# A two-layer decoder on one core: y laid down as it is read, gelus behind the next sines, the queries' modulation in portions, z products at attention's begin, splits one by one

## The chip, the cores and the metric

One core of a Trainium2 chip runs the whole program. The metric is the device time of one execution in microseconds; three runs of a kernel are compared by their median.

## The reference

A sequence of 1024 tokens of width 1024 goes through a state-space layer and an attention layer. In short form (`rms` normalises, `mod` gives shift, scale and gate as c's product with a weight):

```
h = rms(x) * (1 + scale_a) + shift_a
u, z = split(h @ w_in)
y = ssm(u) + D * u                  # 64 groups of 16 channels, 64 complex states each
y = gelu(y)
y = y * sigmoid(y @ w_glu + b_glu) * silu(z)
x = x + gate_a * (y @ w_out)
h = rms(x) * (1 + scale_kv) + shift_kv
k, v, f_logit = split(h @ kv_w);  k = head_rms(k);  F = cumsum(log_sigmoid(f_logit))
h = rms(x) * (1 + scale_b) + shift_b
q, z = split(h @ w_in_b);  q = head_rms(q) / 8
s = q @ k.T + F_q - F_k, causal;  o = softmax(s) @ v        # 16 heads of 64
x = x + gate_b * ((o * silu(z)) @ w_out_b)
```

All is float32.

## The kernel before

Every float32 operand of a large product is split into a high part (`hi`, `aH`, `w_hi`, `wvh`) and the rest (`lo`, `aL`, `w_lo`, `wvl`), and a product is three passes over PE: high by high, low by high, high by low. `split` does this: ACT copies the high part (L94), DVE or POOL subtracts (L102). Weights come in strips through `weight_strip`: SP loads `w_raw`, then it is split.

The program runs through stages. A warm-up of PE (`wu`, L267) stands ahead of the first data. Then come the products u and z of the first layer. The mixer goes over eight tiles of channels, `e` = 0 to 7, each with its taps, products by rotating factors, a scan on DVE, and the way back. In each turn of its loop `tables` gives cosine and sine of the next tile (two calls of ACT's Sin, L596 and L597, from a table that ACT must load), `rotate_back` turns the scan's result (DVE, L213), and `states_out` makes y of the tile on PE (`py`, L700 and L701), puts it through the gelu on ACT in two halves (L703, from another table) and writes it from POOL's queue to the DRAM tensor `y_d` (L704). Later the eight tiles are read back twice by SP, as `yl` for the products with w_glu (`pj_g`) and as `yt` for the gate. On the chip a tile has its 128 partitions as 8 groups of 16 channels and 8 positions of a chunk; `y_rows` reads them back in another order, channel by position:

```
y_d[e].rearrange("(i c) (g k) -> (c g) i k", c=GC, k=NCH)
```

After the products with w_out (`pj_o`), x stands in eight tiles of 128 channels. Then six jobs follow one another, `v0`, `v2`, `k0`, `k2`, `q0`, `q2`: each takes two strips of 256 columns of the weights for values, keys or queries, and makes eight tiles of 128 tokens from each (`tkps`, 24 products of PE per tile, in PSUM buffers `psa`, of which there are three). Values go to DRAM. Keys and queries get a norm by head: ACT squares (L955), DVE sums (L956), POOL takes the power (L957, L958), DVE multiplies (`hnt`, L960); then PE transposes four tiles (`trps`) and the result goes to DRAM in two parts. `modulated` makes the operands of a job from x: DVE normalises and scales (`hmod` or x itself, L184), ACT adds the shift and rounds (`aH`, L185), DVE gives the rest (`aL`, L186). For values and keys this is done at the values' start, for queries at the head of job `q0`. The scale and shift come from vector products on DVE (`gemv`, L141), one per tile of 128 weights that `mod_load` brings in, at every second tile of the jobs `v2` to `k2`.

`z_strips_b` makes the gate's products z of the second layer (`zb`). It is a generator: each `next` emits the three products of one k. Attention walks over 64 steps (16 heads, four blocks of 256 queries); `ahead` makes scores and softmax of a step two steps ahead (`sp`, `mx`, `pr`), `values` transposes the weights (`tp`), splits them (`pth` on ACT, `ptl` on DVE) and multiplies with v (`ov`); `ob` and `oc` collect a step's result. Between steps `some_fill` takes products from `z_strips_b`, and when these are done from `first_rows`, which makes the first output rows (`f`) and needs the gated heads split by `split_o`.

A scheduler orders the instructions of each engine from the order of the code; `tc.issue_after(x)` holds what stands in it behind the instruction x.

## Time and profile before

| | us |
|---|---|
| median of 3 runs | 1188.87 (1187.64 to 1189.01) |
| profiled execution | 1188.02 |
| its span | 1186.2 |
| PE busy | 1148.3 |
| DVE busy | 845.9 |
| ACT busy | 607.1 |
| POOL busy | 318.6 |

The span runs from the first to the last instruction of the profiled execution; the time has 1.8 us around it. Busy times are those in which an engine has an instruction under way, without register and semaphore work; PE is TensorE, DVE VectorE, ACT ScalarE, POOL GpSimd and SP the engine that issues most transfers.

### The profile page before, as it was taken

Reading aid. Unit: us, or ns where it says so; the run is one execution under the profiler, and the core shown is the slowest. Engines: PE = TensorE matmul, PEld = TensorE weight load, DVE = VectorE, ACT = ScalarE, POOL = GpSimd, SP = SyncE. Lnnn points to the kernel's source line nnn. Section 1 sums busy time; section 2 is a strip of 40 time slices with the busy share of each in tenths; the row PEclk is TensorE's granted clock in tenths of the full one; section 3 lists DMA queues with packets and bytes.
Section 4 is the critical chain, followed back from the end, with each engine's and each line's share of the span. In section 5 each row is a group of like instructions: output and inputs, shape, how many; then the busy total and the mean of one; then the engine's idle time right before and its main releaser. Section 6 shows DMA issues by size and latency. Waiting matters only on the chain.

```text
span 1186.2 us, 20506 instructions
## 1 busy us (share of the span) xinstructions
PE 1148.3 (97%) x7486; PEld 1017.5 (86%) x7486; DVE 845.9 (71%) x1713; ACT 607.1 (51%) x1141; POOL 318.6 (27%) x524
## 2 busy tenths in 40 slices
PE   8999999999999999899998999999999999999998
PEld 7688888888888887899997999988988889888786
DVE  7769899887789775934668764458788888887421
ACT  6655776666435323423233342237777776885210
POOL 2300000000000243211343354345555454543100
PEclk8999999999999999999999999989999999999999
DMA  9664566596975872255765473436456564741242
GB/s 360 212 195 118 135 174 170 149 233 196 328 245 198 295 239 86 101 194 181 230 193 176 163 228 109 124 125 143 108 126 137 113 137 101 155 90 45 97 160 72
DMA packets 108099, 197.09 MB, mean 166 GB/s; under 512 B 16832, under 2 KB 57984, under 8 KB 106464
## 3 DMA queue, kind: packets, MB, share of 16 engines
q1 hardware_dynamic: 101104, 174.17, 50.1%
q0 software_dynamic: 5152, 16.85, 3.7%
q10 hardware_dynamic: 1744, 4.77, 1.7%
q8 instruction: 59, 0.97, 0.4%
q14 instruction: 40, 0.33, 0.1%
HBM read 138.21 MB, written 46.27 MB: 156 GB/s over the span
## 4 chain that ended last, share of the span: by engine, by line
PE 77%; DVE 11%; ACT 7%; issue 3%; DMA 2%; SPq 0%; ACTq 0%; DVEq 0%
PE tkps L931 22%; PE pj_g L113 8%; PE u L261 7%; PE pj_o L113 6%; PE zb L113 6%; PE pj_f L113 5%; PE tp L1157 4%; PE ov L1163 2%; PE ov L1164 2%; PE z L261 2%; PE sp L1125 2%; PE f L113 2%; PE sp L1126 2%; ACT pr L1132 2%; DVE ptl L1160 1%
## 5 line engine op out<-in xcount | busy, mean ns | idle before, releaser
L931 PE MATMUL tkps<-wvh,aH 128*128 128x256 f32 (+1 forms) x768 | 219.7, 286 | 6.3 <-DVE hnt L960 3.1
L931 PE MATMUL tkps<-wvl,aH 128*128 128x256 f32 (+1 forms) x768 | 216.1, 282 | 0.0
L931 PE MATMUL tkps<-wvh,aL 128*128 128x256 f32 (+1 forms) x768 | 215.9, 281 | 0.0
L931 PEld LDWEIGHTS tkps<-wvh,aH 128*128 128x128 f32 x768 | 144.4, 188 | 8.0 <-ACT aH L185 3.8
L931 PEld LDWEIGHTS tkps<-wvl,aH 128*128 128x128 f32 x768 | 144.7, 188 | 0.3 <-issue 0.2
L931 PEld LDWEIGHTS tkps<-wvh,aL 128*128 128x128 f32 x768 | 144.2, 188 | 0.6 <-issue 0.2
L1134 POOL TENSOR_SCALAR pr<-pr,sm 128x128 f32<-128x128 f32 (+7 forms) x128 | 96.6, 762 | 85.4 <-DVE sm L1133 84.0
L1159 ACT ACTIVATE pth<-tp 128x512 fp32r<-128x512 f32 (+1 forms) x192 | 87.2, 489 | 55.9 <-PE ov L1163 32.2
L1132 ACT ACTIVATE pr<-pr,mx 128x128 f32<-128x128 f32 (+7 forms) x128 | 98.9, 773 | 24.3 <-DVE mx L1129 22.8
L1160 DVE TENSOR_TENSOR ptl<-tp,pth 128x512 fp32r<-128x512 f32 (+1 forms) x192 | 101.2, 551 | 10.5 <-ACT pth L1159 9.4
L94 ACT ACTIVATE w_hi<-w_raw 128x1024 fp32r<-128x1024 f32 x48 | 50.7, 1056 | 80.8 <-PE pj_f L113 28.6
L1129 DVE CUSTOM_DVE_ANT_0 pr<-sp,msk 128x512 f32<-128x512 f32 (+3 forms) x128 | 72.7, 569 | 23.1 <-PE tp L1157 20.3
L955 ACT ACTIVATE hsq<-tkps 128x256 f32<-128x256 f32 x64 | 24.6, 384 | 125.8 <-PE tkps L931 118.0
L1157 PE MATMUL tp<-ident,pr 128*128 128x128 f32 x576 | 84.9, 276 | 2.2 <-DVE ptl L1160 2.1
L1163 PE MATMUL ov<-pth,vhl 128*128 128x256 f32 x320 | 84.8, 298 | 0.3
L1164 PE MATMUL ov<-ptl,vhl 128*128 128x256 f32 x320 | 80.1, 284 | 1.8 <-DVE ptl L1160 1.7
L1157 PEld LDWEIGHTS tp<-ident,pr 128*128 128x128 f32 x576 | 69.4, 142 | 13.5 <-DVE ptl L1160 4.6
L1125 PE MATMUL sp<-kk,qs 128*128 128x256 f32 (+2 forms) x192 | 71.9, 377 | 2.6 <-DVE mx L1129 2.4
L958 POOL TENSOR_TENSOR hms<-hms,nhalf 128x4 f32<-128x4 f32 x64 | 67.8, 1060 | 5.3
L1126 PE MATMUL sp<-kk,q 66*128 66x256 f32 (+2 forms) x192 | 66.7, 351 | 0.0
L1163 PEld LDWEIGHTS ov<-pth,vhl 128*128 128x128 f32 x320 | 60.5, 189 | 3.2 <-DVE oc L1170 2.0
L1164 PEld LDWEIGHTS ov<-ptl,vhl 128*128 128x128 f32 x320 | 60.7, 190 | 3.0 <-DVE ptl L1160 2.8
(346 smaller groups left out, 3110.0 us busy)
## 6 DMA issues: line engine op xcount, KB each, us to landing
modw<-modw SPq DMA_DIRECT2D x48, 512.0 KB, 3.9
wvr<-kvq_w SPq DMA_DIRECT2D x12, 1024.0 KB, 5.7
w_raw<-a_w_in SPq DMA_DIRECT2D x16, 512.0 KB, 5.6
v_d<-vt POOLq DMA_DIRECT2D x32, 256.0 KB, 3.2
kk<-k_d SPq DMA_DIRECT2D x16, 512.0 KB, 6.6
vhl<-v_d SPq DMA_DIRECT2D x16, 512.0 KB, 8.2
qs<-q_d SPq DMA_DIRECT2D x32, 256.0 KB, 5.0
w_raw<-a_w_out SPq DMA_DIRECT2D x10, 512.0 KB, 5.4
```

The source lines that it names most:

```text
L113: m = T.matmul(ps, w[wt][:, k, :], act[at][k][half], start=(k == k0 and n == 0), stop=(k == k1 and n == 2)).ins
L261: m = T.matmul(ps[:, 0:c1 - c0], w[wt][:, k, :], act[at][k][i][:, c0:c1], start=(k == 0 and n == 0), stop=(k == KT - 1 and n == 2)).ins
L931: T.matmul(ps[:, 0:nv], at, wt[:, k, 0:nv], start=(n == 0), stop=(n == 3 * KT - 1))
L1125: T.matmul(sp[:, 0:wm_], qsl, kk[:, 0, lo:lo + wm_], start=True, stop=False)
L1126: T.matmul(sp[:, 0:wm_], q1_[:, P * i:P * i + P], kk[0:HD + 2, 1, lo:lo + wm_], start=False, stop=True)
L1132: S.activation(pr[:, 0:nk], pr[:, 0:nk], AF.Exp, scale=-1.0, bias=mx, accum_out=sm)
L1134: G.tensor_scalar(out=pr[:, 0:nk], in0=pr[:, 0:nk], scalar1=sm, scalar2=0.0, op0=ALU.mult, op1=ALU.add)
L1157: T.transpose(out=tp[:, b, :], in_=prs[qi][:, P * (b0 + b):P * (b0 + b) + P], identity=ident)
L1159: S.activation(pth[:, 0:m, dst], tp[:, 0:m, :], AF.Copy)
L1160: V.tensor_tensor(out=ptl[:, 0:m, dst], in0=tp[:, 0:m, :], in1=pth[:, 0:m, dst].bitcast(F32), op=ALU.subtract)
L1163: T.matmul(ov, vhl[:, b, :], pth[:, b - b0, :], start=(b == 0), stop=False)
L1164: end = T.matmul(ov, vhl[:, b, :], ptl[:, b - b0, :], start=False, stop=(b == nb - 1)).ins
```

## The change

- The warm-up has 38 calls instead of 28.
- `y_d` gets the order in which it is read. A tile is written in eight transfers of 16 partitions, each laid out by channel; the reads are plain. The first column of `r1` is cleared by DVE instead of POOL.
- `states_out` holds its gelus behind the sine of the next tile (`b_.get("sin")`), and behind them the table for sines is loaded ahead.
- `modulated` is cut into `mod_norm` and `mod_parts`. For the queries, two normalisations follow each tile of job `k2`'s first half, and the splits follow the tiles of `k2`'s second half and of `q0`'s first. The vector products follow every tile of `v2` and `k0`.
- The splits of `b_wz` wait for job `q0`'s end. The z products that stood among the queries and between the first scores are placed as 8 parts in `q2`, 5 behind each of the first two steps' scores and 3 behind each of the next two's.
- `first_rows` calls `split_o` once per part (three times at first) instead of all twelve at once, each behind the step's `ob` and `oc`.

```
-            for _ in range(28):
+            for _ in range(38):
...
-        y_d = dram.tile([KT, P, 8 * NCH], F32, name="y_d", tag="y_d")
+        y_d = dram.tile([KT, P, TC, NCH], F32, name="y_d", tag="y_d")
...
-            return y_d[e].rearrange("(i c) (g k) -> (c g) i k", c=GC, k=NCH)
+            return y_d[e]
...
-                S.activation(sT, sT, AF.Sin, scale=tpi)
+                st["sin"] = S.activation(sT, sT, AF.Sin, scale=tpi).ins
...
-                G.memset(r1[:, :, 0:1], 0.0)
+                V.memset(r1[:, :, 0:1], 0.0)
...
-                    S.activation(yb[:, 4 * hb:4 * hb + 4], py, AF.Gelu_apprx_tanh)
-                G.dma_start(out=y_d[e], in_=yb.rearrange("p g k -> p (g k)"))
+                    with tc.issue_after(sin) if sin else ExitStack():
+                        gelu = S.activation(yb[:, 4 * hb:4 * hb + 4], py, AF.Gelu_apprx_tanh).ins
+                if e + 2 < KT:
+                    with tc.issue_after(gelu):
+                        S.preload_act_table_set("trig_and_small")
+                for i in range(TC):
+                    G.dma_start(out=y_d[e, :, i, :].rearrange("(c g) k -> c g k", c=GC), in_=yb[GC * i:GC * i + GC])
...
             def z_strips_b():
-                w = weight_strip(a["b_wz"][0], [P, KT, P], l_eng=G)
+                with tc.issue_after(q0_end[0]), tc.issue_after(q0_end[1]):
+                    w = weight_strip(a["b_wz"][0], [P, KT, P], l_eng=G)
...
-                if job == "q0":
+                if job == "k2":
                     mod_take(last_nt[-1])
                     s_b = mod_scale(48, 56, vec["b_g"], "s_b")
...
-                    act = act_tiles()
-                    for i in range(2):
-                        for k in range(KT):
-                            with tc.issue_after(k0_end):
-                                modulated(x1, k, i, s_b, sh_b, act)
...
+                                with tc.issue_after(end), tc.issue_after(last_sq[-1]):
+                                    if job == "k2" and not i:
+                                        for ii in range(2):
+                                            mod_norm(x_half(n, ii), x_half(n, ii), ii, s_b[:, n:n + 1])
+                                    elif job == "k2":
+                                        mod_parts(x_half(n, 0), sh_b[:, n:n + 1], act_b[0][n][0], act_b[1][n][0])
+                                    elif job == "q0" and not i:
+                                        mod_parts(x_half(n, 1), sh_b[:, n:n + 1], act[0][n][1], act[1][n][1])
-                            if t % 2 and job != "v0":
+                            if job in ("v2", "k0"):
                                 mod_take(end, 1)
                                 mod_load(wide_dma[-1], 8 * KT)
...
-            for k in range(KT - 2):
-                for i in range(2):
-                    split_o(k, i)
+            todo = [(k, i) for i in range(2) for k in range(KT - 2)]
             for i in range(2):
                 ps = f_tile(0, i)
                 for k in range(KT - 2):
+                    for _ in range(3 if (k, i) == (0, 0) else 1):
+                        if todo:
+                            with tc.issue_after(ends[-1][1]), tc.issue_after(ends[-1][2]):
+                                split_o(*todo.pop(0))
                     project_part(ps, wf_(0), act2, i, (k,), 0, KT - 3)
...
         for j in range(LOOK):
-            if j:
-                some_fill(Z_FIRST)
             pend.append(ahead(j))
-        some_fill(Z_FIRST)
+            with tc.issue_after(sp_end[-1]):
+                some_fill(5)
...
+            if j < 2:
+                with tc.issue_after(sp_end[-1]):
+                    some_fill(3)
```

On ACT, near the end of the mixer's loop (`e` = 6; `r_2778` and `r_2836` are the tile's y before and after), the order before was:

```order
L595 ACTIVATE cT<-sT 128x1024
L703 ACT_TABLE_LOAD
L703 ACTIVATE r_2778<-py 128x512
L596 ACT_TABLE_LOAD
L596 ACTIVATE cT<-cT,hpi 128x1024
L597 ACTIVATE sT<-sT,tpi 128x1024
L703 ACT_TABLE_LOAD
L703 ACTIVATE r_2778<-py 128x512
L401 ACTIVATE ez_2818<-z_2_2819 128x32x8
```

and the changed kernel has there:

```order
L599 ACTIVATE cT<-sT 128x1024
L600 ACTIVATE cT<-cT,hpi 128x1024
L601 ACTIVATE sT<-sT,tpi 128x1024
L708 ACT_TABLE_LOAD
L708 ACTIVATE r_2836<-py 128x512 x2
L405 ACTIVATE ez_2883<-z_2_2884 128x32x8
```

The gelu that stood ahead of the cosine, and the two table loads around it, have gone from that place, and both halves stand behind the sine.

On DVE, at the step from keys to queries, this stood in the order before, the beginning of sixteen normalisations of x (`s_b` is the queries' scale):

```order
L956 TENSOR_REDUCE hms<-hsq 128x4
L163 TENSOR_TENSOR s_b<-mod,vecs 128x8
L168 SCALAR_TENSOR_TENSOR s_b<-s_b,vecs 128x8
L169 TENSOR_SCALAR s_b<-s_b 128x8
L184 SCALAR_TENSOR_TENSOR x_0_3167<-x_0_3167,s_b,q2x 128x512
L184 SCALAR_TENSOR_TENSOR x_1_3168<-x_1_3168,s_b,q2x 128x512
L184 SCALAR_TENSOR_TENSOR x_2_3169<-x_2_3169,s_b,q2x 128x512
L184 SCALAR_TENSOR_TENSOR x_3_3170<-x_3_3170,s_b,q2x 128x512
```

and in job `k2` of the changed kernel this (`hnt` is a finished tile of keys):

```order
L969 TENSOR_TENSOR hnt<-tkps,hms 128x256
L981 SCALAR_TENSOR_TENSOR kl<-trps,vecs,kh 128x512
L182 SCALAR_TENSOR_TENSOR x_4_3243<-x_4_3243,s_b,q2x 128x512 x2
L981 SCALAR_TENSOR_TENSOR kl<-trps,vecs,kh 128x512
L969 TENSOR_TENSOR hnt<-tkps,hms 128x256
L182 SCALAR_TENSOR_TENSOR x_5_3244<-x_5_3244,s_b,q2x 128x512 x2
L965 TENSOR_REDUCE hms<-hsq 128x4 x2
L969 TENSOR_TENSOR hnt<-tkps,hms 128x256
L182 SCALAR_TENSOR_TENSOR x_6_3245<-x_6_3245,s_b,q2x 128x512 x2
```

The normalisations have moved to an earlier job, and two of them stand between one tile and the next.

On ACT, in the last heads, the first splits of the gated heads (`aH`) stood like this before, from the step that was collected at 1016 us on:

```order
L1166 ACTIVATE ob<-ov 64x256
L94 ACTIVATE aH_0_12272<-o_t_7020 128x512
L94 ACTIVATE aH_0_12274<-o_t_7021 128x512
L1159 ACTIVATE pth<-tp 128x4x128
L1159 ACTIVATE pth<-tp 128x128
L1159 ACTIVATE pth<-tp 128x2x128
L1166 ACTIVATE ob<-ov 64x256
L94 ACTIVATE aH_0_12276<-o_t_8320 128x512
```

and stand like this in the changed kernel, eight steps later:

```order
L1193 ACTIVATE ob<-ov 64x256
L94 ACTIVATE aH_0_12344<-o_t_7412 128x512
L94 ACTIVATE aH_0_12346<-o_t_7413 128x512
L94 ACTIVATE aH_0_12348<-o_t_8392 128x512
L94 ACTIVATE aH_0_12350<-o_t_8393 128x512
L1186 ACTIVATE pth<-tp 128x4x128
L1159 ACTIVATE pr,sm<-pr,mx 128x640
L1186 ACTIVATE pth<-tp 128x128
```

Four splits stand in one piece ahead of the next step's `pth`, and DVE's halves (`aL`) stand likewise ahead of its `ptl`.

## Rows read from the trace of the kernel before

**Rows 1.** The page's first part: engine, busy us (share of the span), instructions.

```profile
PE 1148.3 (97%) x7486; PEld 1017.5 (86%) x7486; DVE 845.9 (71%) x1713; ACT 607.1 (51%) x1141; POOL 318.6 (27%) x524
```

**Rows 2.** The table of busy times by stretch of the span: from and to in us, length, then the busy time and count of instructions of PE, PEld, DVE, ACT and POOL, the granted clock of PE (1.00 is full), the share of the DMA engines and GB/s.

```profile
125.00:290.00 165.00, 154.41 (x1130) 138.23 (x1129) 142.03 (x168) 109.92 (x168) 5.14 (x15) 0.99 0.65 180
290.00:457.00 167.00, 167.00 (x725) 134.61 (x724) 126.13 (x173) 66.74 (x92) 21.80 (x21) 1.00 0.73 244
457.00:490.00 33.00, 28.69 (x153) 23.40 (x152) 30.68 (x36) 15.78 (x24) 13.42 (x13) 1.00 0.26 83
...
640.00:656.00 16.00, 10.47 (x71) 9.16 (x70) 16.00 (x27) 5.79 (x11) 4.16 (x4) 1.00 0.18 67
...
802.00:1017.00 215.00, 213.71 (x1398) 191.02 (x1396) 175.38 (x563) 161.70 (x384) 111.95 (x199) 1.00 0.59 129
1017.00:1053.00 36.00, 34.45 (x214) 29.15 (x213) 33.91 (x100) 29.38 (x69) 16.31 (x30) 1.00 0.46 103
1053.00:1072.00 19.00, 17.19 (x113) 15.02 (x112) 16.36 (x42) 13.65 (x29) 9.76 (x16) 1.00 0.38 85
1072.00:1112.00 40.00, 38.35 (x234) 32.35 (x234) 26.61 (x72) 21.80 (x50) 11.91 (x25) 1.00 0.15 46
```

**Rows 3.** The list of waits of PE over the whole span: what waited, what it waited for, us in total, times, the longest.

```profile
PE pk L641 <- DVE moa L213: 5.0, 6, 1.7
PE tkps L931 <- DVE hnt L960: 3.1, 1, 3.1
PE py L701 <- DVE r L213: 3.1, 3, 1.7
PE tkps L931 <- ACT aH L185: 2.8, 2, 1.5
PE sp L1125 <- DVE mx L1129: 2.4, 6, 0.7
PE zb L113 <- DVE aL L186: 2.4, 1, 2.4
```

**Rows 4.** The same kind of table as rows 2, cut where the granted clock changes.

```profile
9.81:12.51 2.70, 1.02 (x4) 0.66 (x4) 2.37 (x3) 1.92 (x4) 0.00 (x0) 1.00 1.02 410
12.51:19.34 6.83, 6.55 (x18) 4.56 (x17) 6.42 (x11) 5.67 (x8) 0.11 (x1) 0.50 1.03 410
...
131.97:135.38 3.41, 3.41 (x10) 2.63 (x9) 3.31 (x5) 2.20 (x6) 0.61 (x1) 0.50 0.79 302
790.00:794.16 4.16, 3.11 (x20) 2.25 (x19) 2.47 (x11) 2.05 (x6) 2.06 (x4) 1.00 0.00 0
794.16:800.98 6.82, 6.82 (x25) 5.59 (x25) 5.80 (x19) 4.94 (x13) 2.70 (x7) 0.50 0.67 231
```

**Rows 5.** The mixer: one row of the list of waits from 125 to 290 us, then rows of the timelines of ACT and of DVE around 265 us (start, length, engine, line, operation, in brackets the idle time before it and what ended it). L703 is the gelu, L596 the cosine, L213 a product on DVE.

```profile
DVE r L213 <- ACT cT L596: 9.7, 6, 4.4
...
262.63 1.28 ACT L703 ACT_TABLE_LOAD   x1
263.93 0.60 ACT L703 ACTIVATE r<-py 128x512 f32<-128x512 f32 x1
264.54 1.28 ACT L596 ACT_TABLE_LOAD   x1
...
267.02 1.22 DVE L213 TENSOR_TENSOR r<-cT,v 128x1016 f32<-128x1016 f32 x1 [4.36 <-ACT cT L596]
```

**Rows 6.** y on its way through DRAM: POOL's cleared columns (125 to 300 us), the time to landing in the view of y's DRAM tensor, and the last tile's write on POOL's timeline and its first read on SP's.

```profile
L677 POOL MEMSET r<- 128x8 f32 x7 | 0.8, 113 | 164.8 <-PE py L701 164.8
...
DMA to landing us min/median/max: 2.9/3.9/6.7
...
284.46 0.53 POOL L704 DMA_DIRECT2D y_d<-r  x1 [13.69 <-ACT r L703]
...
287.40 0.37 SPq L787 DMA_DIRECT2D yl<-y_d  x1
```

**Rows 7.** Groups of instructions from 463 to 490 us, on POOL and on DVE: line, engine, operation, tiles, shape, count | busy us, mean ns | idle before.

```profile
L102 POOL TENSOR_TENSOR w_lo<-w_raw,w_hi 128x1024 fp32r<-128x1024 f32 x2 | 4.8, 2398 | 3.4 <-ACT w_hi L94 3.3
...
L184 DVE SCALAR_TENSOR_TENSOR hmod<-x,s_kv,q2x 128x512 f32<-128x512 f32 x10 | 13.9, 1428 | 0.0
```

**Rows 8.** The step from keys to queries: a group on DVE from 636 to 656 us, and rows of PE's timeline.

```profile
L184 DVE SCALAR_TENSOR_TENSOR x<-x,s_b,q2x 128x512 f32<-128x512 f32 x16 | 10.9, 745 | 0.0
...
645.66 0.39 PE L931 MATMUL tkps<-wvh,aH 128*128 128x256 f32 x1 [3.11 <-DVE hnt L960]
...
648.58 0.27 PE L967 MATMUL trps<-ident,hnt 128*128 128x128 f32 x1
```

**Rows 9.** Groups on DVE from 500 to 640 us, values and keys.

```profile
L141 DVE CUSTOM_DVE_ANT_0 modw<-modw,c_b 128x1024 f32<-128x1024 f32 x16 | 19.4, 1210 | 0.0
...
L956 DVE TENSOR_REDUCE hms<-hsq 128x4 f32<-128x256 f32 x21 | 8.7, 417 | 8.0 <-ACT hsq L955 7.9
L960 DVE TENSOR_TENSOR hnt<-tkps,hms 128x256 f32<-128x256 f32 x20 | 8.4, 421 | 11.7 <-POOL hms L958 11.5
...
L972 DVE SCALAR_TENSOR_TENSOR kl<-trps,vecs,kh 128x512 fp32r<-128x512 f32 x8 | 5.6, 747 | 0.7 <-ACT kh L971 0.7
```

**Rows 10.** A group on DVE from 990 to 1121 us: the splits of the gated heads.

```profile
L102 DVE TENSOR_TENSOR aL<-o_t,aH 128x512 fp32r<-128x512 f32 x16 | 12.4, 783 | 2.9 <-ACT aH L94 2.8
```

**Rows 11.** A group on PE from 0 to 41 us: the warm-up.

```profile
L267 PE MATMUL wu<-onesm 128*128 128x128 f32 x56 | 8.7, 331 | 1.1 <-POOL onesm L66 1.1
```

More of the change, by code (lines that the diff above doesn't have):

```diff
@@ L102, in split, with act_tiles @@
             parts[:] = h, (l_eng or V).tensor_tensor(out=lo, in0=x, in1=hi.bitcast(F32), op=ALU.subtract)
-        def act_tiles(more=0):
-            return [[[apool.tile([P, HL + more * i], F32R, name=f"a{p}{k}_{i}", tag=f"a{p}{k}_{i}") for i in range(2)]
-                     for k in range(KT)] for p in "HL"]
+        def act_tiles(more=0, halves=(0, 1)):
+            return [[[apool.tile([P, HL + more * i], F32R, name=f"a{p}{k}_{i}", tag=f"a{p}{k}_{i}") if i in halves else None
+                      for i in range(2)] for k in range(KT)] for p in "HL"]
         def project_part(ps, w, act, half, ks, k0=0, k1=KT - 1):
@@ L1029, in trunk, with x_half @@
                     V.tensor_scalar(out=gate_b, in0=gate_b, scalar1=0.5, scalar2=None, op0=ALU.mult)
-                    act = act_tiles()
-                    for i in range(2):
+                elif job == "q0":
+                    act = act_tiles(0, (1,))
+                    for p in range(2):
                         for k in range(KT):
-                            with tc.issue_after(k0_end):
-                                modulated(x1, k, i, s_b, sh_b, act)
-                    lx.close()
-                    modx.close()
-                    at0 = top.enter_context(tc.tile_pool(name="at0", bufs=2, side="right", reuse_waits="tile"))
-                    o_t = [at0.tile([P, L], F32, name=f"o_t{e}", tag=f"o_t{e}", bufs=1) for e in range(2)]
+                            act[p][k][0] = act_b[p][k][0]
+                def x_half(k, i):
+                    return x1[k][:, HL * i:HL * i + HL]
                 src = a["kvq_w"]
@@ L1042, in trunk @@
                 for i in range(2):
+                    if job == "k2" and i:
+                        act_b = act_tiles(0, (0,))
+                    elif job == "q0" and i:
+                        lx.close()
+                        modx.close()
+                        at0 = top.enter_context(tc.tile_pool(name="at0", bufs=2, side="right", reuse_waits="tile"))
+                        o_t = [at0.tile([P, L], F32, name=f"o_t{e}", tag=f"o_t{e}", bufs=1) for e in range(2)]
                     for d in range(2):
@@ L1175, in trunk @@
             steps += [(2 * p + h, c) for h, c in ORDER]
-        hds = {}
-        ocs = {}
+        hds, ocs, sp_end = {}, {}, []
         def ahead(j):
```

46 lines of the change are left out of this document (25 added, 21 removed).

## The prediction

> **What bounds the kernel now.** I read the page first, for the busy shares: PE works 1148.3 us of the 1186.2 us span, 97% [rows 1]. So PE is the bound, and a change that leaves PE's work alone can give back at most what PE does not do: 37.9 us of idle time, and the work that it does at the lower clock. Next I read the table by stages, for where those 37.9 us lie [rows 2]: the reader is to see that the mixer's stretch from 125 to 290 us has 10.6 us of them (165 less 154.41) and the start of the values 4.3 us (33 less 28.69), that the sixteen us around the step from keys to queries have 5.5 us with DVE busy for all 16.00, and that the last heads (1017 to 1072) have 3.4 us. From 290 to 457 PE has none. Third, PE's list of waits, for who ends them [rows 3]: nearly always DVE, with one late operand each. Last, the granted clock [rows 4]: three stretches at 0.50, that is 1.2 instead of 2.4 GHz: 6.83 us at the first products, 3.41 us in the mixer, 6.82 us at the first scores. PE had waited just before: 1.68 us of idle time in the 2.70 us ahead of the first, 1.05 in the 4.16 us ahead of the last.
>
> The sum starts from the profiled execution, 1188.02 us; the median of the runs, 1188.87, lies 0.85 us above it.
>
> **The longer warm-up.** 28 calls are 56 passes of 8.7 us [rows 11], 0.155 us each, so ten more calls are 3.1 us. They cover the idle 1.6 us behind the warm-up and run 1.5 us into the time when the first data are there. What follows is paced by DVE, which is busy 6.42 of the 6.83 us at the low clock [rows 4], so a faster PE there mostly waits. Bounds: 1.5 us lost (the delay is not caught up), 1.5 us gained (the idle time saved). I take 0.5 us gained.
>
> **y laid down as it is read.** One write per tile becomes eight; the sixteen reads have long pieces instead of pieces of 128 elements. POOL issues such a transfer in 0.53 us [rows 6], so eight take 4.2 us and the last is issued 3.7 us later than the single one was. POOL has nothing else to do there. The write of tile 7 is what counts: it was issued at 284.46 us, and SP asked for the tile at 287.40 [rows 6]. The seven tiles ahead give PE products to do, and from 290 us PE never waited [rows 2]; how much slack tile 7 had, no row says. Bounds: 0, and 3.7 us lost. I take 0, for the shorter read gives part of it back. The cleared column (0.113 us, eight times) goes from POOL to DVE: 0.9 us, counted in the next part.
>
> **Gelus behind the next sines.** This is the largest term. In the mixer DVE waited 9.7 us in six places for ACT's cosine [rows 5]. The last place shows why: ACT loads a table (1.28 us), does a gelu (0.60), loads the sines' table (1.28) and only then the cosine, while DVE stands for 4.36 us. With the gelu behind, 3.16 us of this go, and 1.2 stay. The other five waits together are 5.3 us, some 1.1 each, less than those 3.16, so I let them go wholly. DVE gains 9.7 - 1.2 = 8.5 us, less the 0.9 us of the cleared columns: 7.6. The number of table loads stays at 19; a load for the sines now stands behind the gelu in ACT's order, ahead of the next evictions. PE gets what it waited for DVE: pk 5.0 and py 3.1 us [rows 3] of the 10.6 idle in the stretch, and the 3.41 us at half clock cost it 1.7 at most. Bounds: 2.5 us (only the first and largest waits turn into PE time, as gelus and loads delay the evictions of z) and 8.5 us. I take 6.0, some four fifths of DVE's 7.6, as PE and DVE don't wait at the same places throughout.
>
> That first row of ACT's also bears on a price. A load began at 262.63 and the gelu at 263.93: 1.30 us from one to the other [rows 5]. The Trainium skill ("ScalarE: Activation LUTs", What ACT_TABLE_LOAD costs) gives a drain of some 1.38 us beside the load, 2.66 us per switch. By that the two switches and the gelu would be 5.9 us, the last wait would go wholly as well, and the sum would be some 1 us lower. The rows show no room for such a drain.
>
> **The start of the values.** Two splits of the z weights leave: ACT's share, and on POOL two of 2.40 us each, while DVE's normalisations beside them average 1.428 us [rows 7] against 0.745 for the same form elsewhere [rows 8]. Ten at that difference are 6.8 us of DVE, some of it beside other POOL work that stays. PE waited 2.8 us for aH here, which hangs on these [rows 3]. I take 2.7 us, nearly all of it; bounds 1.5 and 4.3 (all idle time of the stretch).
>
> **The queries' modulation in portions.** Before, 16 normalisations in one piece (10.9 us of them inside the stretch [rows 8]) stand on DVE ahead of the tile that PE waits for: 3.1 us for hnt and 2.4 us for aL [rows 3], with all of DVE's 16.00 us taken [rows 2]. Now two come behind each tile of k2's first half and the splits behind the next two half jobs. A tile is 24 products, 2.9 us from the first to the transposes behind it (645.66 to 648.58) [rows 8]. DVE's work per tile is then 0.42 (squares' sum), 0.42 (hnt), 1.49 (two normalisations) and about 0.4 for kl [rows 9]: 2.7 us, just under the tile, and the weights' split comes to that; three PSUM buffers take up a lag of a tile. The same holds for k0, where the vector products of 1.21 us now follow each tile. I take 5.0 of the 5.5 us, bounds 3 and 5.5.
>
> **z products at attention's begin.** The number of products is unchanged. Instead of filling the queries' jobs, they stand between the first scores, where PE waited for mx: 1.05 us of idle time from 790 to 794.16, and 6.82 us ran at half clock [rows 3, 4], worth 3.4 us if PE alone was the bound. DVE was busy 5.80 of those 6.82. I take 1.0 + 2.5 = 3.5 us, bounds 0 (the clock falls at another place) and 4.4.
>
> **Splits one by one.** Here the order speaks against the change. Before, twelve splits stood singly or in pairs over 1017 to 1053 us, where PE lost 1.55 us; two heads without them lose some 0.2 [rows 2]. So 1.3 us come back. But now they wait for the step before the first product that needs them, and stand four, two, two, two and two behind one another within the five steps that were at 1058 to 1082 us, beside the split of a weight. Each takes DVE 0.78 us [rows 10]: 9.4 us. DVE's free time there: 2.64 us in 19 and 13.4 in 40 [rows 2], so about 1.9 + 3.3 = 5.2 in these 24. Over 4 us don't fit; scores run two steps ahead, which hides some 2.4 of them. I take 1.8 lost less 1.3 gained: 0.5 us lost. Bounds: 1.3 gained, 2.8 lost.
>
> **The sum.** -0.5 + 0 - 6.0 - 2.7 - 5.0 - 3.5 + 0.5 = -17.2, so 1170.8 us against 1188.02, and 1171.6 on the scale of the runs' median. A measurement tells about 0.2% from no change here, 2.4 us.
>
> **Rivals.**
> - *The mixer and the clock keep what they have.* The gelus and loads behind the sines hold the evictions of z instead, and the low clock only moves: 2.5 instead of 6.0 and 0 instead of 3.5, so 1171.6 + 7.0 = 1178.6. For it: ACT is busy 109.92 of 165 us there, and just as many loads remain. Against it: PE's long waits name DVE. Chance 0.17.
> - *The stall of the values' start moves along.* POOL's two splits of 2.40 us now stand in q2 between the powers that hnt waits for, and PE waits again: 2.7 given back, 1174.3. Against it: a tile's lag of 2.8 us fits into the PSUM buffers. Chance 0.08.
> - *All idle time goes.* 1.5, 8.5, 4.3, 5.5, 4.4 and 1.3 gained: 25.5, so 1163.4. Chance 0.09.
> - *Slower: the pieces of tile 7 land one after another.* If each of the eight holds up the next for a landing, the tile comes 7 landings later: at the median of 3.9 us [rows 6] that is 27.3 us, so 1171.6 + 27.3 = 1198.9. It decides from 2.8 us per piece (7 of them make the 17.2 and 2.4 more). Against it: POOL's issue takes 0.53 us of the 2.9 to 6.7 that a landing takes [rows 6], and the next issue needs nothing from the one before. Chance 0.05. The Trainium skill ("DMA: Bandwidth & Descriptors", Rules for kernel authors) speaks on this side: small transfers should be made one, as under 64 KB most of the time is overhead. A piece here is just 64 KB, so by that rule each would keep most of its fixed cost; no run yet shows whether these costs lie beside each other.
> - *It doesn't do what it says:* the gains and the new crowding at the end cancel, within 0.2% of before. Chance 0.04.
>
> **How the numbers follow.** The forecast, 1171.6 us, has 0.57, with a range of its own from 1166 to 1177. For 8 in 10 I go from 1162 to 1181, which takes in the first three rivals. Faster 0.91, the same 0.04, slower 0.05.
>
> **What would show it.** Right: DVE's wait for the cosine falls below 2 us, no PE wait over 1 us from 640 to 656, none for aH at the values' start, a clock of 1.00 at the first scores, PE's idle time near 22 us. Wrong: PE waits for ez's buffers in the mixer, an idle PE at the first product with y's tile 7, PE waits of more than 2 us for ptl in heads 13 and 14.

## The result, and the profile after

The changed kernel takes 1182.09 us (median of five runs, 1181.67 to 1183.26) against 1188.87 us: a ratio of 0.9945, with a 95% interval from 0.9929 to 0.9960. (Here and below the ratio is estimated from all executions of both kernels, so it need not be the quotient of the two medians.) That is faster, by some 0.55%: 6.8 us where 17.2 were forecast, and the median lies 1.1 us above the upper end of the range of 8 in 10, 1181. The profiled execution took 1183.26 us, its span is 1181.1 us, 5.1 us less than before's.

The page's first part of after (engine, busy us, share, instructions), to lay beside [rows 1]:

```profile
PE 1146.0 (97%) x7506; PEld 1018.0 (86%) x7506; DVE 838.3 (71%) x1721; ACT 605.6 (51%) x1141; POOL 349.8 (30%) x572
```

PE has 2.3 us less and DVE 7.6 us less; POOL has 31.2 us more, mainly the 56 more issues of y's pieces. The table by stages of after, with the columns of [rows 2]:

```profile
125.00:290.00 165.00, 153.11 (x1122) 137.54 (x1121) 140.48 (x173) 108.13 (x166) 32.29 (x62) 0.99 0.70 177
457.00:490.00 33.00, 31.86 (x178) 26.80 (x177) 27.11 (x38) 15.12 (x24) 10.25 (x11) 1.00 0.20 72
640.00:656.00 16.00, 16.00 (x138) 16.00 (x138) 11.54 (x23) 5.25 (x12) 6.49 (x10) 1.00 0.31 118
656.00:790.00 134.00, 129.82 (x1023) 125.90 (x1022) 66.86 (x136) 50.40 (x93) 59.65 (x89) 0.99 0.47 146
790.00:802.00 12.00, 12.00 (x71) 10.45 (x70) 9.04 (x32) 8.22 (x21) 5.44 (x9) 1.00 0.54 134
1053.00:1072.00 19.00, 15.17 (x86) 12.32 (x85) 17.32 (x42) 12.25 (x27) 9.74 (x14) 0.91 0.19 55
```

Read against [rows 2], the first number behind the length (PE busy) tells the story. Three stages did what they should: at the values' start PE's idle time is 1.1 instead of 4.3 us, from 640 to 656 us it is nothing instead of 5.5, and the first scores have neither idle time nor a low clock. Three others got worse: the mixer has 11.9 us idle instead of 10.6, the stretch from 656 to 790 has 4.2 us where there was none, and the last heads have 3.8 us in 19 instead of 1.8. The row of before from 656 to 790 us, which [rows 2] leaves out:

```profile
656.00:790.00 134.00, 134.00 (x1087) 131.19 (x1086) 71.47 (x135) 42.83 (x76) 58.14 (x85) 1.00 0.49 154
```

PE's list of waits names the new ones, with the columns of [rows 3]:

```profile
PE py L705 <- DVE r L217: 7.4, 5, 4.3
PE sp L1151 <- DVE mx L1156: 3.9, 4, 1.8
PE tkps L940 <- DVE hnt L969: 3.3, 2, 2.7
```

The single rows on PE's timeline of after (start, length, engine, line, operation, in brackets the idle time ahead and what ended it), one from each of the three stages:

```profile
280.91 0.80 PE L705 MATMUL py<-r,moa 128*128 128x128 f32 x2 [4.34 <-DVE r L217]
...
679.92 0.52 PE L940 MATMUL tkps<-wvh,aH 128*128 128x256 f32 x1 [2.67 <-DVE hnt L969]
...
1064.86 0.44 PE L1151 MATMUL sp<-kk,qs 128*128 128x384 f32 x1 [1.84 <-DVE mx L1156]
```

Within 0.9 us of the end of each of the three waits the granted clock falls to 0.50, which is 1.2 GHz. A table of after, cut there (the last row is the stretch of the first data, which had 6.83 us at 0.50 in [rows 4]):

```profile
280.50:284.20 3.70, 3.29 (x16) 3.29 (x17) 1.56 (x3) 0.61 (x1) 0.00 (x0) 0.54 0.57 173
680.00:683.30 3.30, 3.30 (x16) 3.30 (x17) 2.69 (x5) 0.00 (x0) 1.71 (x3) 0.50 0.04 12
1065.50:1069.30 3.80, 3.80 (x13) 3.26 (x14) 2.82 (x12) 3.09 (x9) 2.64 (x5) 0.55 0.51 173
17.80:21.30 3.50, 3.50 (x11) 2.92 (x12) 3.50 (x8) 2.80 (x5) 0.00 (x0) 0.51 1.04 411
```

So the low clock did not go; it moved from the first scores to these places, behind the new waits. It did shrink: before had four stretches of it, 20.5 us in all (a fourth, from 56.88 to 60.29 us, is not in [rows 4]), after has four of 3.4 us, 13.7 in all.

A ledger shows where the time went in one profiled execution of each kernel. Each row is a point in the program, read from the timelines: for before the time at which it is reached, for the others the difference to before in us (negative is earlier). "Scan e" is the end of DVE's scan for tile e, the others are starts on PE or ends on DVE. The columns e5 to e8 belong to the experiments below.

| point | before | after | e5 | e6 | e7 | e8 |
|---|---|---|---|---|---|---|
| scan 0 | 109.14 | +0.80 | -0.24 | -1.16 | +0.33 | -0.60 |
| scan 4 | 203.87 | -3.88 | -4.92 | -5.68 | -3.62 | -5.48 |
| scan 6 | 251.08 | -2.90 | -3.94 | -4.53 | -2.52 | -4.23 |
| scan 7 | 273.01 | -2.38 | -4.50 | -5.11 | -2.88 | -3.46 |
| last `py` | 283.26 | +2.49 | -1.40 | +0.14 | -0.50 | -2.86 |
| last `pj_o` | 473.23 | +2.48 | +3.02 | +2.82 | -0.50 | -2.04 |
| last tile of values | 573.66 | -1.90 | -1.30 | -1.55 | -4.97 | -6.35 |
| `oc` of step 8 | 845.28 | -7.54 | -7.17 | -9.78 | -10.64 | -14.39 |
| `oc` of step 42 | 1006.38 | -7.62 | -7.19 | -9.80 | -10.66 | -14.43 |
| end | 1186.25 | -5.10 | -4.72 | -6.21 | -12.66 | -16.46 |

After gains 3.9 us up to scan 4 and is 2.5 us late when the mixer ends: it gives back 6.4 us in the last three turns. DVE's waits in the mixer (125 to 292 us of after, columns as in the list of waits) say what for:

```profile
DVE sT L217 <- DMA v<-v: 10.9, 5, 6.5
...
DVE r L217 <- ACT cT L600: 1.2, 1, 1.2
```

The wait for the cosine fell from 9.7 us to 1.2 [rows 5], exactly as worked out. In its place stands `v<-v`, the transfer that exchanges the two halves of the scan's result: 10.9 us, where before it was 3.3 us in one place. Before's row of the same list, and the place on DVE's timeline of before:

```profile
DVE sT L213 <- DMA v<-v: 3.3, 1, 3.3
...
277.54 1.23 DVE L213 TENSOR_TENSOR sT<-sT,v 128x1024 f32<-128x1024 f32 x1 [3.27 <-DMA v<-v]
```

The two places that count, and the one cosine left, on DVE's timeline of after:

```profile
256.20 1.23 DVE L217 TENSOR_TENSOR sT<-sT,v 128x1024 f32<-128x1024 f32 x1 [3.24 <-DMA v<-v]
...
264.24 1.22 DVE L217 TENSOR_TENSOR r<-cT,v 128x1016 f32<-128x1016 f32 x1 [1.15 <-ACT cT L600]
...
278.38 1.23 DVE L217 TENSOR_TENSOR sT<-sT,v 128x1024 f32<-128x1024 f32 x1 [6.48 <-DMA v<-v]
```

The 3.2 us won at the last tile's cosine (4.36 in [rows 5], now 1.15) were lost 8 us earlier, on the 3.24 us of a swap that had not been waited for. At the last tile the swap takes 6.48 us instead of 3.27, and the half clock behind it costs some 1.7 more (an estimate: half of the 3.42 us at 0.50): 3.2 and 1.7 are the 4.9 us by which the ledger falls from scan 7 to the last `py`. The queue that issues the swap, SP's timeline of after:

```profile
266.27 0.53 SPq L408 DMA_DIRECT2D z_d<-ez  x1
267.17 0.94 SPq L796 DMA_DIRECT2D yl<-y_d  x2
268.20 0.37 SPq L86 DMA_DIRECT2D w_raw<-a_w_glu  x1
270.66 1.22 SPq L587 DMA_DIRECT2D v<-v  x2
```

Two reads of y and a strip of w_glu, 512 KB each, are issued 3.5 to 2.5 us ahead of the swap. Before, one read of y and the strip went out at 268.61 and 269.07 us, 4.4 and 4.0 us ahead of a swap at 273.04 (SP's timeline of before):

```profile
268.61 0.37 SPq L787 DMA_DIRECT2D yl<-y_d  x1
269.07 0.66 SPq L86 DMA_DIRECT2D w_raw<-a_w_glu  x1
273.04 1.16 SPq L583 DMA_DIRECT2D v<-v  x2
```

The scan moved forward by more than the loads, so the swap now comes closer behind 1.5 MB, where 1.0 MB stood further ahead.

### The profile page after: what moved, and what is told of

It reads as the page before. It is cut to its first block, busy times and chain, and to the rows that moved or that the text cites. A ratio compares the mean times of both kernels' runs of the same rounds, so it can differ in the third digit from the quotient of the medians.

```text
span 1181.1 us, 20618 instructions
## 1 busy us (share of the span) xinstructions
PE 1146.0 (97%) x7506; PEld 1018.0 (86%) x7506; DVE 838.3 (71%) x1721; ACT 605.6 (51%) x1141; POOL 349.8 (30%) x572
## 4 chain that ended last, share of the span: by engine, by line
PE 73%; DVE 9%; ACT 7%; DMA 6%; issue 3%; POOL 1%; SPq 0%; ACTq 0%; DVEq 0%
PE tkps L940 22%; PE pj_g L113 8%; PE pj_o L113 7%; PE zb L113 6%; PE pj_f L113 5%; PE u L265 5%; PE tp L1184 4%; PE ov L1190 3%; DMA v<-v 3%; PE ov L1191 2%; PE sp L1151 2%; PE sp L1152 2%; PE f L113 2%; ACT pr L1159 1%; ACT w_hi L94 1%
## 5 line engine op out<-in xcount | busy, mean ns | idle before, releaser
L713 POOL DMA_DIRECT2D y_d<-r x64 | 33.4, 552 | 200.2 <-ACT r L708 199.1
L967 POOL TENSOR_TENSOR hms<-hms,nhalf 128x4 f32<-128x4 f32 x64 | 70.8, 1106 | 5.3
L265 PE MATMUL z<-aH,w_hi 128*128 128x258 f32 (+2 forms) x192 | 62.7, 327 | 1.4 <-ACT ez L405 1.4
```

The lines of the kernel that those rows point to most:

```text
L265: m = T.matmul(ps[:, 0:c1 - c0], w[wt][:, k, :], act[at][k][i][:, c0:c1], start=(k == 0 and n == 0), stop=(k == KT - 1 and n == 2)).ins
```

## The experiments

The theory that came out of the ledger: the mixer's gain is real, and is given back by the last swap, late because of SP's order, with the clock behind it. Its rivals: the eight pieces on POOL's queue make the swap late; or the gelus' move is itself worth nothing. Of the queries' and the last heads' new waits the theory is that the order of PE's products and the crowding on DVE make them.

Each kernel is the changed one with the edit shown. They were timed in three groups, each beside runs of the kernel before on the same chip (medians 1189.16, 1189.14 and 1189.21 us): e1 to e4, e5 to e8, and e9 to e12, each group on a chip of its own. Medians of different groups are therefore compared with some care.

| kernel | median us | ratio to before, interval |
|---|---|---|
| after | 1182.09 | 0.9945 (0.9929 to 0.9960) |
| e1 y in one write | 1182.76 | 0.9942 (0.9922 to 0.9962) |
| e2 gelus as before | 1185.51 | 0.9965 (0.9948 to 0.9981) |
| e3 both | 1182.83 | 0.9942 (0.9922 to 0.9963) |
| e4 splits as before | 1181.72 | 0.9931 (0.9909 to 0.9953) |
| e5 swap first | 1181.06 | 0.9931 (0.9911 to 0.9950) |
| e6 queries' splits in twos | 1181.79 | 0.9938 (0.9923 to 0.9954) |
| e7 e4 and a split on POOL | 1176.95 | 0.9905 (0.9887 to 0.9923) |
| e8 e5, e6 and e7 | 1172.96 | 0.9867 (0.9848 to 0.9885) |
| e9 e8, mixer as before | 1176.97 | 0.9882 (0.9857 to 0.9908) |
| e10 e8 without e5 | 1175.51 | 0.9881 (0.9858 to 0.9903) |
| e11 e8, y in one write | 1174.00 | 0.9865 (0.9840 to 0.9890) |
| e12 e8, warm-up of 28 | 1172.60 | 0.9858 (0.9835 to 0.9881) |

**e1, y in its old layout and one write.**

```
-        y_d = dram.tile([KT, P, TC, NCH], ...)
+        y_d = dram.tile([KT, P, 8 * NCH], ...)
-            return y_d[e]
+            return y_d[e].rearrange("(i c) (g k) -> (c g) i k", c=GC, k=NCH)
-                for i in range(TC):
-                    G.dma_start(out=y_d[e, :, i, :]..., in_=yb[GC * i:GC * i + GC])
+                G.dma_start(out=y_d[e], in_=yb...)
```

> The changed kernel with y's DRAM tensor and its one write per tile as before; everything else as changed. Theory P (the eight pieces of tile 6 fill the queues while the two transfers that swap the halves of the last scan are under way): the wait of DVE for the swapped half in the last turn, 6.5 us in the changed kernel, falls to 2 to 3 us, PE's wait of 4.3 us before the last py to under 1.5, the clock stays at full there, and the time falls by 4 to 6 us, to 1176 to 1178. Theory G (the gelus and table loads behind the sines cost this, the pieces don't): the wait stays above 5 us and the time within 1 us of 1182.

1182.76 us: no gain. The swap's wait is 5.30 us and `py` then waits 5.46 us, so taking the pieces off POOL's queue does not make the swap early: of the two expectations theory G came.

**e2, the gelus in their old place, y's pieces kept.**

```
-                    with tc.issue_after(sin) if sin else ExitStack():
-                        gelu = S.activation(..., AF.Gelu_apprx_tanh).ins
-                if e + 2 < KT: ... preload_act_table_set
+                    S.activation(..., AF.Gelu_apprx_tanh)
```

> The changed kernel with the gelus where they stood before (ahead of the next sines, with no table loaded ahead); y in eight pieces stays. Theory P: y's pieces of tile 6 go out earlier relative to the last swap or at the same place, so the last wait for the swapped half stays over 4 us in part, and DVE's waits for the cosine are back at 8 to 10 us; time 1183 to 1187. Theory G: the last wait goes to 2 to 3 us, waits for the cosine are back, time 1179 to 1182.

1185.51 us, slower than after. The cosine's wait is back at 9.3 us in six places, the last swap's wait falls to 4.5. The gelus' move thus does take the cosine's wait away, and the swap's grows where the cosine's shrinks. Time and waits are those that theory P named here, which e1 had refuted; e3 settles it, for without the pieces its swap is waited for just as long.

**e3, both edits of the mixer undone.** (The column that DVE clears and the 38 calls of the warm-up stay, so it is not quite the mixer of before.)

> The changed kernel with both of these as before, so that the mixer is that of before. It gives the worth of all the other parts: the last py at 283 to 285 us instead of 286.0, and a time of 1178 to 1181 if the mixer's two edits together lose 2 to 3 us, as the traces of before and after say. If they gain (the forecast: 6 us), the time is over 1183.

1182.83 us, 0.7 us from after, and the two intervals overlap. What the mixer's two edits bring together in the changed kernel, forecast as 6 us, these runs can't tell from nothing. The last swap is waited for 4.56 us, as in e2 (4.50), and `py` then waits 2.88.

**e4, the twelve splits at once, as before.**

```
-            todo = [(k, i) for i in range(2) for k in range(KT - 2)]
+            for k in range(KT - 2):
+                for i in range(2):
+                    split_o(k, i)
...
-                        if todo: ... split_o(*todo.pop(0))
```

> The changed kernel with the twelve splits of the gated heads asked for at once, as before. Theory T (the crowding of splits in heads 13 and 14 costs what the spread over heads 11 and 12 didn't): the four waits of PE between 1058 and 1067 us (3.8 us in all) and the half clock behind them (some 1.7 us) go, 1.4 us of small waits come back some 30 us earlier; net 2 to 4 us faster, 1178 to 1180. If the wait at that place is due to the split of the third output weight alone (as in the kernel before, 1.7 us), the time is within 1 us of 1182.

1181.72 us, alike by the medians, as the second expectation had it; in the trace the part behind step 42 takes 1.4 us longer than before the change, that of after 2.5. One long wait is left there, and the rows on DVE ahead of it show its cause (e4's timeline of PE, then that of DVE):

```profile
1063.80 0.58 PE L1191 MATMUL ov<-ptl,vhl 128*128 128x256 f32 x1 [1.68 <-DVE ptl L1187]
```

```profile
1061.47 1.67 DVE L102 TENSOR_TENSOR wf<-w_raw,wf 128x1024 fp32r<-128x1024 f32 x1
1063.06 0.68 DVE L1187 TENSOR_TENSOR ptl<-tp,pth 128x512 fp32r<-128x512 f32 x1
```

The split of an output weight, 1.67 us in one piece, stands on DVE just ahead of the `ptl` that PE needs. Before the change PE's list of waits had the same wait, 1.7 us for `ptl` at `ov`, once.

**e5, the last swap ahead of the two reads of y and the strip of w_glu on SP.**

```
-                with tc.issue_after(loaded[-1]):
+                with tc.issue_after(last_swap[0] if k >= 4 else loaded[-1]):
                     last_y = ...                      # the reads yl
...
-            wg = [weight_strip(a["a_w_glu"][e], [P, KT, P], V) for e in range(2)]
+            with tc.issue_after(last_swap[0]):
+                wg = [weight_strip(a["a_w_glu"][e], [P, KT, P], V) for e in range(2)]
```

> The changed kernel with one difference on SP's queue: the two transfers that swap the halves of the last scan are issued ahead of two reads of y (512 KB each) and the first load of w_glu (512 KB), not behind them. Theory Q (the swap is slow because 1.5 MB were queued just ahead of it, and the earlier DVE ends its scan the closer it stands behind them): the time from the scan's end to the product that needs the swap, 7.75 us in the changed kernel, falls to 4 to 5 us; PE's wait of 4.3 us before the last py falls to 1 to 2 and the half clock behind it (1.7 us) goes; the values start 3 to 5 us earlier, time 1177 to 1179. Theory W (only y's eight writes of the tile before, from POOL, fill the engines): the swap still takes 6.5 us or more, time within 1.5 us of 1182.

1181.06 us. The swap is issued at 268.55 and waited for 4.57 instead of 6.48 us, and the mixer ends 1.4 us earlier than before, 3.9 us earlier than in after. By its median e5 is where theory W put it, within 1.5 us of 1182; from the scan's end to the product that needs the swap it took 5.8 us, between what the two theories had. At the last `pj_o` all that the mixer gained is gone in this execution (ledger: +3.02). PE's timeline of e5 and a table of the stretch behind show where:

```profile
382.91 0.50 PE L113 MATMUL pj_o<-aH,w_lo 128*128 128x512 f32 x1 [2.04 <-DVE w_lo L102]
```

```profile
383.60:387.00 3.40, 3.40 (x10) 2.62 (x9) 3.40 (x6) 3.40 (x7) 0.00 (x0) 0.50 0.84 295
```

The low part of a strip of w_out comes late. On DVE its split stands behind gate work, and that work waited longer for its reads of z: 15.9 us in ten places between 290 and 470 us, 12.8 us in nine in after. That these reads are the cause is read from the order; it was not tried by itself. Then the clock falls. [rows 2] had no idle PE from 290 to 457 us, so this is a new wait. It belongs to this execution and not to the edit: e8, whose instructions up to the last `pj_o` stand in the same order on every engine, comes there at -2.04, and between 290 and 457 us PE waits in it once, 0.53 us. e5's profiled execution, 1183.38 us, was the slowest of its six (1178.01 to 1183.38).

**e6, the queries' splits in twos.** The splits of two tiles follow each of the first four tiles of a half job, instead of one behind each of eight.

```
-                                    elif job == "k2":
-                                        mod_parts(x_half(n, 0), ...)
+                                    elif job == "k2" and n < 4:
+                                        for m in (2 * n, 2 * n + 1):
+                                            mod_parts(x_half(m, 0), ...)
```

(and the same in `q0`)

> The changed kernel with the queries' splits two per tile in the first half of each half job, instead of one per tile up to its end. In the order, PE's first tiles of q0 are then no longer interleaved three at a time. Theory I (PE waits 2.7 us at 680 us because three tiles were interleaved and ended together, so that all three PSUM buffers wait for one chain of squares, powers and products): the waits for hnt at 680 and 707 us (2.7 and 0.6) and the half clock from 680 to 683 (1.6) go, 4 to 5 us faster, 1177 to 1179. Theory L (DVE's load in k2 and q0 is too high, whatever the order): waits for hnt of 2 us or more stay there or come earlier, time 1181 to 1184.

1181.79 us. After's wait of 2.67 us has its cause in DVE's rows (timeline of after): three sums of squares one behind another, for three tiles that ended together.

```profile
677.35 0.42 DVE L965 TENSOR_REDUCE hms<-hsq 128x4 f32<-128x256 f32 x1 [1.11 <-ACT hsq L964]
678.23 0.42 DVE L965 TENSOR_REDUCE hms<-hsq 128x4 f32<-128x256 f32 x1 [0.46 <-ACT hsq L964]
679.12 0.42 DVE L965 TENSOR_REDUCE hms<-hsq 128x4 f32<-128x256 f32 x1 [0.46 <-ACT hsq L964]
679.45 0.41 DVE L969 TENSOR_TENSOR hnt<-tkps,hms 128x256 f32<-128x256 f32 x1
```

PE's order had mixed the products of three tiles, since the operands came one tile at a time, so all three PSUM buffers were full at once. In e6 the tiles stand one behind another, the waits are 1.35 us twice, and the clock stays at 1.00 there. From the last `pj_o` to step 8, e6 gains 12.6 us on before, after 10.0. This difference holds from execution to execution: the seven kernels without e6's edit (after, e1 to e5, e7) gain 10.0 to 10.7 us there, the six with it (e6, e8 to e12) 11.5 to 12.7. So the edit is worth some 2 us. The median does not show it and is where theory L put it; the profiled execution gave back 2.7 us in the products with w_glu and w_out, where after, with the same instructions up to there, gave back nothing.

**e7, e4 and that weight's split on POOL.**

```
-                split(raw, *wf[e])
+                split(raw, *wf[e], None, G)
```

> As e4 (the twelve splits asked for at once), and the low part of the third output weight is made by POOL instead of DVE. Theory T: the wait of 1.7 us for ptl at 1064 us goes as well, and nothing new comes: 1.5 to 2 us faster than e4, 3 us faster than the changed kernel, 1179. Theory B (POOL's 2.4 us hold up the scaling of the softmax weights and so the next transposes): a wait for tp or ptl of 1 us or more stays, time as e4.

1176.95 us, 4.8 us under e4. The end of the kernel takes 3.4 us of this: 1.7 for the wait and some 1.5 for the 3.1 us at half clock that followed it in e4 (first row e4, second e7):

```profile
1053.00:1072.00 19.00, 17.19 (x103) 15.20 (x102) 15.12 (x43) 13.32 (x31) 9.49 (x16) 0.91 0.22 69
```

```profile
1053.00:1072.00 19.00, 18.77 (x123) 16.55 (x122) 17.33 (x52) 14.41 (x34) 10.45 (x19) 1.00 0.22 70
```

This too holds: behind step 42 the six kernels with e7's edit (e7 to e12) gain 1.8 to 2.1 us on before, e4 loses 1.4, and the six with the splits as after has them (after, e1 to e3, e5, e6) lose 2.5 to 4.2. The rest is not e7's edit: the mixer, whose instructions are the same in after, e4, e6 and e7, ended at +2.5, +2.7, +0.1 and -0.5 us in these four executions.

**e8, the edits of e5, e6 and e7 together.**

> e5, e6 and e7 together. If the three causes are independent: 4 + 4 + 3 = 11 us less than the changed kernel, some 1171 to 1173, which is the forecast's time; if one of them only moves its stall, 1174 to 1177.

1172.96 us: 0.9867 of before, 9.1 us faster than after. PE's busy time is 1140.8 us, 5.2 less than after's with the same 7506 instructions; the granted clock is 1.00 throughout. Of the 11.4 us by which e8's ledger ends ahead of after's, 4.6 stand behind step 42 (e7's edit), 2.3 between the last `pj_o` and step 8 (e6's), and 4.5 ahead of the last `pj_o`, of which e10 will tell e5's part. The swap's wait is 3.71 us and `py`'s 1.81:

```profile
277.06 0.49 PE L707 MATMUL py<-r,moa 128*128 128x128 f32 x2 [1.81 <-DVE r L217]
```

**e9, e8 with the mixer as before** (the edits of e3 added).

> The kernel of e8 with the mixer's two edits undone (gelus in their old place, one write of y per tile). Theory M, that these edits are worth what the trace of after showed by the fifth scan (3.9 us) once the last turn no longer gives it back: 1176 to 1177 us, DVE's waits for the cosine back at some 9 us. Theory N, that a later limit (the loads of the products with w_glu and w_out) takes whatever the mixer gains: 1172 to 1174 us, with y's end some 3 us later than in e8 and the end of pj_o no later.

The median, 1176.97, speaks for 4 us, the profile against it: its execution took 1172.01 us, and the mixer ends at -2.13 us, 0.7 us behind e8. Two of the six executions took 1172.0 us at a mean granted clock of 0.999 and 1.000, four took 1176.8 to 1178.5 at 0.994 to 0.996. What the mixer's edits are worth here, between 0.4 and 4 us, is left open.

**e10, e8 without e5.**

> The kernel of e8 without the moved swap: SP's order at the mixer's end is that of after. If the order on SP costs what the trace of e5 showed at y's end (3.9 us): 1175.5 to 1177 us. If the order is worth only what the medians of after and e5 differ by (1.0 us): 1173.5 to 1174.5 us. If the swap's wait is a matter of the transfers under way and not of the order: 1173 us, and the wait for the halves 3.7 to 6.8 us as from run to run of the same order.

1175.51 us: 2.6 us behind e8 in the medians and 3.1 in the profiled executions. The swap's wait is 6.17 us and `py`'s 3.67; the rows on DVE of e8 and then of e10:

```profile
274.52 1.23 DVE L217 TENSOR_TENSOR sT<-sT,v 128x1024 f32<-128x1024 f32 x1 [3.71 <-DMA v<-v]
```

```profile
277.93 1.23 DVE L217 TENSOR_TENSOR sT<-sT,v 128x1024 f32<-128x1024 f32 x1 [6.17 <-DMA v<-v]
```

The intervals of e8 and e10 overlap, and e8 ran on another chip. But e12, on e10's chip and apart from the warm-up the kernel of e8, is 2.9 us ahead, with four of its five executions below e10's fastest. So SP's order is worth some 2.6 to 2.9 us here, as the first expectation had it at its lower end; the third, 1173 us, falls by the time. Its waits don't refute it: 6.17 us lies in its span, and e12, with the swap first, waits 5.05.

**e11, e8 with y in one write** (the edit of e1 added).

> The kernel of e8 with y in its old layout and one write per tile. Theory: the eight pieces load POOL's queue in the mixer's last turns and cost about 1 us (the difference of e1's trace to after's): 1171.5 to 1172.5 us. Rival: the plain reads pay for the pieces, as the medians of after and e1 (1182.09 and 1182.76) say: 1173 to 1174 us.

1174.00 us, 1.0 us behind e8 by the medians, and alike by the ratios, 0.9865 and 0.9867. What its profiled execution lost (1175.20 us, of 1172.53 to 1175.25) is on PE's timeline of e11, and in the table's row of the stretch behind:

```profile
293.65 0.50 PE L113 MATMUL pj_g<-aH,w_hi 128*128 128x512 f32 x1 [1.01 <-ACT aH L788]
...
296.15 0.50 PE L113 MATMUL pj_g<-aH,w_hi 128*128 128x512 f32 x1 [1.05 <-ACT w_hi L94]
```

```profile
296.90:300.30 3.40, 3.40 (x9) 2.63 (x9) 1.06 (x2) 3.37 (x4) 0.00 (x0) 0.50 0.97 359
```

y arrives late (`aH` here is made from `yl`), PE waits twice, and the clock falls; the mixer had ended 1.4 us earlier than e8's, and the last `pj_o` starts 2.5 us later. The time is that of the rival, that the plain reads pay for the pieces, but its lead over the first expectation is within the spread of these five executions, and e5 shows how much a single one can lose in this stretch. Whether the pieces gain anything is left open.

**e12, e8 with 28 calls in the warm-up.**

> The kernel of e8 with 28 calls in the warm-up, as before the change. If the ten more calls only push the first products back (msy was 0.8 us later after the change): 1172.0 to 1172.5 us. If they keep the granted clock up at the first products (e8 had no stretch at 0.50 there, before had 6.83 us of it): the stretch at 0.50 is back between 12 and 20 us and the time is 1173 to 1175 us.

1172.60 us, no difference from e8. A stretch at 0.50 is there, from 15.6 to 19.0 us, and costs nothing that can be seen: scan 0 ends 0.4 us later than e8's. It is not clear that the calls make it: after and e2, with 38 of them, had such a stretch as well, and e6, with 38, had none.

## Why the prediction failed, step by step

| part | predicted | from the ledger |
|---|---|---|
| warm-up | -0.5 | +0.8 |
| mixer with y | -6.0 | +1.7 |
| values' start | -2.7 | -4.4 |
| queries and attention's begin | -5.0 - 3.5 | -5.6 |
| splits | +0.5 | +2.4 |
| sum | -17.2 | -5.1 |

The right column is of one execution of each kernel, and up to the last `pj_o` five executions of the same instructions (after, e4, e6, e7 and e10) lie up to 3.3 us apart. So the signs of the first two rows say little; but from scan 0 to the last `py` none of the eight kernels with both of the mixer's edits gains more than 2.3 us, where 6.0 were forecast.

**Gelus behind the sines: the step that failed.** The mechanism was right to the tenth on DVE, 9.7 to 1.2 us. The term for PE, 6.0 us gained, was wrong: after against e3 shows 0.7, not clear of nothing. The step that failed is "PE gets what it waited for DVE": it asked what DVE had waited for and not what it would wait for then. The halves' swap is under way while DVE waits for the cosine; with the cosine early the swap ends last. Its 10.9 us, 7.6 more than before, take back most of the 8.5 gained, and the half clock behind the last wait takes more. Some of it hangs on SP's order at the mixer's end, which e10 and e12 show to be worth some 2.6 to 2.9 us; that the rest comes of the earlier scan alone is read from the rows. From the swap's issue to the use of its result it took 6.5 to 8.0 us in the six executions in which the loads went out first and the scan came early (after, e1, e4, e6, e7, e10), and 4.8 to 6.3 us in the five in which the swap went first (e5, e8, e9, e11, e12). With the gelus in their old place and 1.0 MB ahead of the swap it took 4.5 to 5.8 us (before, e2, e3). The Trainium skill ("DMA: Bandwidth & Descriptors", Two DMAs through the same engine are not ordered) says that descriptors of one queue start in order within one DMA engine; the longer times behind loads of 1.0 to 1.5 MB, and e10 against e8, agree. Of the rivals, "the mixer and the clock keep what they have" came nearest, 1178.6, but for another reason: z's evictions cost one wait of 1.4 us (`z` for `ez`, a sign that the prediction had named), the swap the rest. That the clock would move was right. The prediction counted three stretches at 0.50; there were four. Of its signs of being right, four of five came; the fifth did not, for PE's idle time is 35.1 us and not near 22.

**y laid down as it is read** was taken as 0, with a loss of up to 3.7 us. e11 and e1 put it at 1.0 and 0.7 us gained by their medians, neither beyond its interval. PE never waited from 290 to 457 us of after, though tile 7's first read went out at 297.07 instead of 287.40 us. The slower rival, pieces one after another, is refuted by the view of y's tensor in after (first for the sixteen writes behind 262 us, then for the eight of tile 7):

```profile
DMA to landing us min/median/max: 2.3/3.9/6.9
```

```profile
DMA to landing us min/median/max: 2.3/2.3/2.7
```

POOL issues the eight within 4.16 us and each lands 2.3 to 2.7 us behind its issue; the single write took 2.9. (The prediction read the 2.9 to 6.7 us of [rows 6] as those of a write; the view holds reads of y as well, and the eight writes alone took 2.9 to 5.6.) So the costs of these eight pieces lay beside each other. The Trainium skill's advice against transfers of under 64 KB ("DMA: Bandwidth & Descriptors", Rules for kernel authors), cited in the forecast, did not decide here.

**Values' start:** right in kind, too small; the whole of the stall for `aH` went, as the upper bound had it, and 1.14 us for a weight's high part are left. That the stall moves along came only in small: the two splits of z's weights stand on POOL at 725 and 736 us now, and only PE's 0.37 us for `hnt` at 740 lie behind one of them.

**Queries' portions:** the 5.5 us went, and 2.67 + 0.64 + 0.37 us of waits for `hnt` and 3.4 us at half clock came in `q0`. The prediction counted DVE's work per tile and let three PSUM buffers take up a lag; it did not look at the order of PE's products, in which three tiles ran abreast and filled all three. With the order of e6 the longest wait halves and the half clock goes.

**Attention's begin** came out as said: 12.00 of 12.00 us busy at full clock.

**Splits one by one:** 2.4 us lost lie within the bound of 2.8, not at the 0.5 taken. The waits are at the steps forecast, on `mx` and `ptl` behind the splits. The 1.2 us of the weight's split among them were mentioned and not priced. Undoing the order of the twelve gave back 1.2 us (e4), moving this one 3.4 more (e7), so it was the larger item; moving it alone was not tried.

**The warm-up:** within its bounds and too small to tell. Ten more calls made it 1.5 us longer (10.18 against 8.67 us), not 3.1: the 0.155 us for a pass was a mean over passes of 0.21 us at the start and 0.11 us behind.

## What to carry over

When a wait of an engine goes, list what else that engine's next instruction needs and when each of these arrives: the transfer that ended just behind is the next bound, and when its producer comes earlier, it may meet other traffic on its queue. When operands are handed out in small portions, look at how the consumer's order mixes tiles, and whether all buffers then fall due at once. Judge small repairs together: e8 gained 9.1 us on after, where its parts alone (e5, e6 and e7) had shown 1.0, 0.3 and 5.1, each uncertain by some 2 us. And judge an edit by its own stretch of the ledger over many kernels: the worth of e6 and e7 stands out there, while their medians hide it or show too much.

## What the hardware showed unexpectedly

A short wait of PE cost more than itself here: in after, waits of 1.84 to 4.34 us came with 3.4 us at a granted clock of 0.50, worth up to 1.7 us each by estimate. But not always: 3.03 us in e7, 3.65 in e2 and 3.67 us in e10, at the same `py`, were followed by none, while 2.46 us in e12 were. And a stretch of 3.4 us at 0.50 from some 55 to 57 us on is in ten of the fourteen traces, before's among them, and not in those of after, e6, e8 and e11. The same instructions thus differ from one execution to the next by some us, in e9 by 6.5, and a profile of one execution can't tell apart edits of two or three.

A stage in which PE never waited ([rows 2], 290 to 457) did not always have time to spare: in e5 and e6 PE came to it 3.9 and 2.4 us earlier than in after, waited there for strips (2.04 us; 0.79 and 0.86 us), and left it no earlier. In e8, with e5's instructions up to there, PE came 1.5 us earlier still, waited 0.53 us, and left it 5.1 us ahead of e5.
